# Trunk kernel: Newton steps with one tensor input, and the first weights of a layer subtracted on another engine

## The chip, the cores and the metric

One core of a Trainium2 chip runs the kernel. The engines are TensorE (PE in the profile; its weight loads PEld), VectorE (DVE), ScalarE (ACT), GpSimd (POOL) and SyncE (SP), which issues most of the DMAs. Each works through its own queue in order. The metric is the device time of one execution in microseconds (us); the kernel before has a median of 1444.65 over 3 runs (1443.39 to 1447.72).

## The reference, cut to what matters

Two decoder layers over 512 tokens of width 1024, batch 1, with a layer norm ahead of them:

```python
def layer_norm(x, g, b):
    mu = jnp.mean(xf, axis=-1, keepdims=True)
    xc = xf - mu
    var = jnp.mean(xc * xc, axis=-1, keepdims=True)
    return xc * lax.rsqrt(var + LN_EPS) * g + b

h = layer_norm(x, ln0_g, ln0_b)
for l in range(DEPTH):
    mix = hybrid_mixer(h, w_in[l], ...)
    h = layer_norm(DEEPNORM_ALPHA * h + mix, ln1_g[l], ln1_b[l])
    xa = memory_cross_attention(h, mem, w_xq[l], w_xkv[l], w_xo[l])
    h = layer_norm(DEEPNORM_ALPHA * h + xa, ln2_g[l], ln2_b[l])
    ff = swiglu(h, w_ffn_in[l], w_ffn_out[l])
    h = layer_norm(DEEPNORM_ALPHA * h + ff, ln3_g[l], ln3_b[l])
```

The mixer projects h to a gated causal convolution (31 taps on 512 channels, then a norm) and to a gated linear attention in chunks of 64 tokens (q, k, v, an output gate r and a decay). The cross-attention takes keys and values from 256 memory tokens, which are the same for both layers. All of it is float32.

## The kernel before

**Precision by halves.** A float32 product is made of three matmuls (`mm3`, L136 to L139): each operand is split into a rounded part and what is left of it. `split` (L100) makes the two: ScalarE copies the rounded part (L101), and VectorE or GpSimd subtracts it from the source (L102). Matmuls L137 and L139 need the rounded part of the activations, L138 their remainder.

**Weights.** `wchunk` (L121) loads 512 KB into one of four `raw` buffers by a DMA from SyncE's queue (L125), and splits it into one of four buffers of a ring (`w_...`). ScalarE's copy therefore waits for the DMA and for TensorE to have left the ring's buffer; the next DMA into the same `raw` buffer waits for the subtraction. Which engine subtracts comes from a list that `wlo_engines` sets and `wlo_next` goes through in turn: (POOL, DVE) at first, POOL from the start of a layer's mixer, (POOL, DVE) again from the middle of it, DVE from the cross-attention on.

**Activations.** Four token tiles h_100 to h_103 of 128 tokens. `out_proj` (L254) multiplies into PSUM banks `po`, adds them to h (L273; this frees the bank), takes statistics (L277) and calls `layer_norm` (L175), which takes the mean off (L184), finds the reciprocal root of the variance, scales (L190), and has TensorE transpose the tile (`lt_ln`, L198) into PSUM; `split` then makes hT_ln, which all projections of the next stage read.

**The reciprocal root.** `rstd_of` (L141) starts from an integer trick (L147) and makes five VectorE steps on numbers with n columns: L154, L157, L154, L159, L160. In the layer norms n is 1, one number for each of 128 partitions, and all five are SCALAR_TENSOR_TENSOR with two tensors in SBUF. In the norm of the attention (n = 8) and that of the convolution (n = 2), L151 and L152 stand for L154.

**A layer's mixer** (loop over l, L539 on). `conv_in(0)` projects the first half of the convolution's channels, in layer 1 in two halves of the tokens, so that its first half needs only h_100 and h_101. Its weights are w_c, four chunks (w_c_100, 101, 110, 111 in layer 1), and its first four matmuls go to four banks; two of them were those of the last h. Then come `conv_taps` (L590: 31 taps per channel tile on VectorE, put behind everything else that is ready, so that they fill its gaps), the decays, `conv_in(1)`, q, k and v, the state S, and `gla_pair` for two token tiles at a time: products `pa`, `po`, the norm (y_rms), og on VectorE (L786) and its transposes `ogt` (L790). `conv_norm` transposes the finished taps (acc, cvt) and normalises them. In layer 0 the memory's keys (`mem_K`, w_xk, KT) come ahead of the layer, beside the input norm; in layer 1 between v and the output gate (pair 0) and behind it (pairs 1 to 3). `mem_V` (w_xv) and the output projection (w_mo) follow.

**The input norm** leaves its gain and bias out of h at first: L525 transposes the plain h, and ScalarE applies the gain on the way to hT_ln (xf, L527). `residual0` (L530) later applies them to h itself, on GpSimd, ahead of v in layer 0.

**The order.** It isn't written by hand. Each engine's queue is set when the program is built, by a planner that simulates how long instructions take; `high_priority` moves a stretch forward. An edit in one place can thus reorder others.

Of the kernel before, what the change touches and what calls it, by code (L numbers as in the profile page):

```python
# [12 lines left out]
F32 = mybir.dt.float32  # L13
# [4 lines left out]
ALU = mybir.AluOpType  # L18
AX = mybir.AxisListType

P = 128
# [3 lines left out]
NT = T // P  # L25
# [26 lines left out]
def trunk(ctx: ExitStack, tc, a, out):  # L52
# [53 lines left out]
    def wlo_engines(*engs):  # L106
        wlo[0], wlo[1] = engs, 0
# [33 lines left out]
    def rstd_of(v, n, name):  # L141


        y = small.tile([P, n], F32, tag=f"ny{n}", name=f"y_{name}")
        t = small.tile([P, n], F32, tag=f"nt{n}", name=f"t_{name}")
        s = small.tile([P, n], F32, tag=f"ns{n}", name=f"s_{name}")
        DVE.tensor_scalar(y.bitcast(I32), v.bitcast(I32), -0.5, 1597463007.0 - 2.0 ** 31, ALU.mult, ALU.add)  # L147

        def vyy():
            if n > 1:  # L150
                DVE.tensor_mul(t, y, v)  # L151
                DVE.tensor_mul(t, t, y)  # L152
            else:
                DVE.scalar_tensor_tensor(t, y, v, y, ALU.mult, ALU.mult)  # L154

        vyy()
        DVE.scalar_tensor_tensor(y, t, -3.0, y, ALU.add, ALU.mult)  # L157
        vyy()
        DVE.scalar_tensor_tensor(s, t, -40.0 / 3.0, t, ALU.add, ALU.mult)  # L159
        DVE.scalar_tensor_tensor(y, s, 80.0, y, ALU.add, ALU.mult)  # L160
        return y

    def bcast_row(dst, src_row, n, q):
# [2 lines left out]
    def load_gb(g, b, name, q=nc.sync):  # L166
        gb = block([P, 2, D], F32, f"gb_{name}")
        bcast_row(gb[:, 0, :], g, D, q)
        bcast_row(gb[:, 1, :], b, D, q)
        return gb  # L170
# [301 lines left out]
    def new_K(l):  # L472
        return [block([P, NK, MEM], F32R, f"KT{j}_{l}") for j in range(2)]

    def mem_K(l, mT, KT, pr):
        proj_feat(a["w_xkv"][l], mT,
                  [(pr * 256, 256, lambda m, ps: split(KT[0][:, pr * 2 + m, :], KT[1][:, pr * 2 + m, :], ps))],
                  f"xk{pr}_{l}", n=MEM)
# [10 lines left out]
    def load_x(*tts):  # L489
        for tt in tts:  # L490
            nc.sync.dma_start(h[tt], a["x"][0, tt * P:(tt + 1) * P, :])
# [7 lines left out]
    lncol = const.tile([P, 2 * NK], F32, name="lncol")  # L499
    DVE.tensor_copy(lncol, pl[:, :2 * NK])  # L500
    KT = new_K(0)
    mem_K(0, mT, KT, 0)
    load_x(0, 1)
    mem_K(0, mT, KT, 1)
    load_x(2, 3)
# [21 lines left out]
            ACT.activation(xf, pt, AF.Identity, scale=lncol[:, k:k + 1], bias=lncol[:, NK + k:NK + k + 1])  # L527
            split(hT[0][k // 4][:, k % 4, :], hT[1][k // 4][:, k % 4, :], xf)

    def residual0():  # L530
        gb = load_gb(a["ln0_g"], a["ln0_b"], "ln0")
        for tt in range(NT):
            POOL.tensor_mul(h[tt], h[tt], gb[:, 0, :])
            POOL.tensor_add(h[tt], h[tt], gb[:, 1, :])

# [3 lines left out]
    for l in range(L):  # L539
# [14 lines left out]
        DVE.tensor_scalar(nba, chan[:, 0:2, CW + 3], -1.0, None, ALU.mult)  # L554
        gnorm = chan[:, 0, CW + 4:CW + 5]
        mov = mov_hT(hT)
        wlo_engines(POOL)


        u = block([P, 4, T], F32, n_("u"))  # L560
# [73 lines left out]
            DVE.tensor_copy(dec, qe[:, :, CH - 1::CH])  # L634

        conv_in(0)
        if l > 0:
            mT = mem_T(f"{l}")
            KT = new_K(l)
# [13 lines left out]
        for hp in range(2):  # L653
            pt = bank(n_(f"kdt{hp}"), tag="tr")
            for tt in range(NT):
                PE.transpose(pt[:, tt * P:(tt + 1) * P], kd[:, hp, tt * P:(tt + 1) * P], ident)
            ACT.activation(kdT[:, hp].rearrange("p a b -> p (a b)"), pt, AF.Copy)
        if l == 0:
            residual0()
        v = block([P, NT, 512], F32, n_("v"))  # L660
        run(proj_tok(w_in, mov, 1536, lambda tt, ps: ACT.activation(v[:, tt, :], ps, AF.Copy), n_("v")))

        S = block([P, NCH, 2, P], F32, n_("S"))
        for g in range(2):
            pus = [bank(n_(f"pu{g}{ci}"), tag="tr").rearrange("p (c h e) -> p c h e", c=2, h=2) for ci in range(2)]
# [126 lines left out]

        V = new_V(l)
        if l > 0:
            mem_K(l, mT, KT, 0)
        gla_pair(0)
        run(proj_r)
        wlo_engines(POOL, DVE)  # L800
        for pr in range(1, 4) if l > 0 else ():
            mem_K(l, mT, KT, pr)
        for c in range(2):
# [125 lines left out]
```

## Time and profile before

| | |
|---|---|
| median of 3 runs | 1444.65 us |
| the profiled execution | 1448.14 us |
| its span | 1446.4 us |
| TensorE's mean granted clock | 0.992 |
| TensorE's clock, 720 to 740 us | 0.74 |
| TensorE's clock, 860 to 880 us | 0.91 |
| VectorE busy, 700 to 720 us | 18.50 of 20 us |
| VectorE busy, 820 to 840 us | 20.00 of 20 us |

Layer 0 begins at about 38 us, layer 1 at about 722. A row of a timeline gives start, duration, engine, line, operation, tiles and shapes, how many instructions it groups (x), and in brackets the idle time of the engine before it with what ended it. Numbers in tiles' names are left out in such rows. The granted clock is the share of full speed that TensorE's throttle let through.

### The profile page before, as it was taken

How to read it: one execution, taken by the hardware profiler on the slowest of the kernel's cores; microseconds unless marked ns; L12 is line 12 of the kernel's file. 1: busy time of each engine (PE TensorE's matmuls, PEld its weight loads, DVE VectorE, ACT ScalarE, POOL GpSimd, SP SyncE). 2: the span in 40 equal slices, each digit the busy share in tenths (PEclk: the TensorE clock that was granted, in tenths of full speed). 3: DMA queues.
4: the chain of work that ended last, by engine and by line, in shares of the span. 5: the costliest groups of instructions: out<-in, count | busy, mean ns of one | idle time of the engine just before them, and what ended most of it. 6: DMA issues, size and time to landing. Idle time of an engine off the chain costs nothing.

```text
span 1446.4 us, 22112 instructions
## 1 busy us (share of the span) xinstructions
PE 1405.3 (97%) x8943; PEld 1257.2 (87%) x8943; DVE 1015.9 (70%) x1674; ACT 608.8 (42%) x976; POOL 218.8 (15%) x124
## 2 busy tenths in 40 slices
PE   8999999999999999999979999999999999999997
PEld 7787878988999899899877888889889998998996
DVE  6699977557877367466859997685578664763767
ACT  5553362442555155245225335424424542561550
POOL 3467230000000000000133423300000000000000
PEclk9999999999999999999989999999999999999999
DMA  7423250221365265545242323612214662643641
GB/s 248 131 79 117 88 190 25 95 86 58 97 161 170 76 168 131 147 113 128 84 126 84 93 85 115 217 59 88 76 51 119 164 190 59 161 135 114 146 132 58
DMA packets 108730, 168.62 MB, mean 117 GB/s; under 512 B 7485, under 2 KB 81937, under 8 KB 108629
## 3 DMA queue, kind: packets, MB, share of 16 engines
q1 hardware_dynamic: 102548, 145.98, 32.1%
q0 software_dynamic: 5760, 20.97, 7.8%
q8 instruction: 70, 1.15, 0.3%
q14 instruction: 32, 0.25, 0.1%
q10 hardware_dynamic: 320, 0.27, 0.1%
HBM read 144.13 MB, written 2.10 MB: 101 GB/s over the span
## 4 chain that ended last, share of the span: by engine, by line
PE 76%; DVE 14%; DMA 5%; ACT 3%; issue 2%; POOL 0%; SPq 0%; DVEq 0%; POOLq 0%; ACTq 0%
DVE cv L590 6%; PE po_fo L137 5%; PE po_fo L138 5%; PE po_fo L139 5%; PE fx L402 5%; PE fx L404 5%; PE fx L403 5%; DMA s<-raw_a 3%; PE fw L404 2%; PE fw L403 2%; PE fw L402 2%; PE pp_xq L137 2%; PE pp_xq L138 2%; PE pp_xq L139 2%; PE po_mo L139 2%
## 5 line engine op out<-in xcount | busy, mean ns | idle before, releaser
L284 POOL DMA_DIRECT2D s<-raw_a x40 | 34.9, 885 | 873.4 <-DVE w_s L102 256.1
L590 DVE SCALAR_TENSOR_TENSOR cv<-u,chan,cv 128x511 f32<-128x511 f32 (+28 forms) x240 | 158.6, 728 | 0.3
L138 PE MATMUL po_fo<-w_fo,ph 128*128 128x512 f32 (+1 forms) x358 | 138.1, 386 | 0.0
L139 PE MATMUL po_fo<-w_fo,pl 128*128 128x512 f32 (+1 forms) x358 | 137.0, 386 | 0.0
L137 PE MATMUL po_fo<-w_fo,ph 128*128 128x512 f32 (+1 forms) x358 | 131.7, 386 | 0.0
L101 ACT ACTIVATE w_a<-raw_a 128x1024 fp32r<-128x1024 f32 x60 | 63.2, 1054 | 150.6 <-PE po_fo L139 124.6
L102 DVE TENSOR_TENSOR w_s<-s,w_s 128x1024 fp32r<-128x1024 f32 x80 | 97.3, 1220 | 33.3 <-ACT w_s L101 33.0
L101 ACT ACTIVATE w_s<-s 128x1024 fp32r<-128x1024 f32 x80 | 83.8, 1052 | 48.0 <-DMA s<-raw_a 27.6
L402 PE MATMUL fx<-T_ln,w_s 128*128 128x256 f32 x320 | 91.6, 287 | 3.5 <-ACT u L415 3.3
L403 PE MATMUL fx<-T_ln,w_s 128*128 128x256 f32 x320 | 91.2, 285 | 0.0
L404 PE MATMUL fx<-T_ln,w_s 128*128 128x256 f32 x320 | 90.6, 285 | 0.0
L273 DVE SCALAR_TENSOR_TENSOR h<-h,po_fo 128x512 f32<-128x512 f32 (+1 forms) x49 | 32.3, 671 | 71.2 <-PE po_fo L139 71.1
L102 DVE TENSOR_TENSOR w_a<-raw_a,w_a 128x1024 fp32r<-128x1024 f32 x60 | 73.0, 1220 | 9.1 <-ACT w_a L101 8.1
L139 PEld LDWEIGHTS po_fo<-w_fo,pl 128*128 128x128 f32 x358 | 67.3, 188 | 13.3
L138 PEld LDWEIGHTS po_fo<-w_fo,ph 128*128 128x128 f32 x358 | 67.3, 188 | 13.0
L137 PEld LDWEIGHTS po_fo<-w_fo,ph 128*128 128x128 f32 x358 | 66.9, 188 | 12.9
L402 PEld LDWEIGHTS fx<-T_ln,w_s 128*128 128x128 f32 x320 | 62.2, 194 | 4.2 <-ACT u L415 3.7
L102 DVE TENSOR_TENSOR w_fo<-raw_fo,w_fo 128x1024 fp32r<-128x1024 f32 x44 | 52.8, 1219 | 13.6 <-ACT w_fo L101 13.6
L403 PEld LDWEIGHTS fx<-T_ln,w_s 128*128 128x128 f32 x320 | 62.2, 194 | 0.0
L404 PEld LDWEIGHTS fx<-T_ln,w_s 128*128 128x128 f32 x320 | 61.8, 194 | 0.0
L138 PE MATMUL pp_xq<-hT_ln,w_xq 128*128 128x256 f32 (+1 forms) x192 | 61.3, 322 | 0.0
L139 PE MATMUL pp_xq<-hT_ln,w_xq 128*128 128x256 f32 (+1 forms) x192 | 60.3, 319 | 0.0
(315 smaller groups left out, 4478.3 us busy)
## 6 DMA issues: line engine op xcount, KB each, us to landing
raw_a<-w_ffn_in SPq DMA_DIRECT2D x60, 512.0 KB
raw_fo<-w_ffn_out SPq DMA_DIRECT2D x44, 512.0 KB
s<-raw_a POOLq DMA_DIRECT2D x40, 512.0 KB, 4.9
s<-w_ffn_in SPq DMA_DIRECT2D x20, 512.0 KB
raw_xk<-w_xkv SPq DMA_DIRECT2D x16, 512.0 KB
raw_c<-w_in SPq DMA_DIRECT2D x16, 512.0 KB
raw_xv<-w_xkv SPq DMA_DIRECT2D x16, 512.0 KB
raw_mo<-w_mix_out SPq DMA_DIRECT2D x16, 512.0 KB
```

The lines of the kernel that those rows point to most:

```text
L101: ACT.activation(hi, src, AF.Copy)
L102: eng.tensor_sub(lo, src, f(hi))
L137: PE.matmul(o, lh, rh, start=start, stop=False)
L138: PE.matmul(o, lh, rl, start=False, stop=False)
L139: PE.matmul(o, ll, rh, start=False, stop=stop)
L273: DVE.scalar_tensor_tensor(h[tt][:, c0:c1], h[tt][:, c0:c1], scale, bks[c][:, :c1 - c0], ALU.mult, ALU.add)
L284: POOL.dma_start(dst, src, accum_op=ALU.add)
L402: PE.matmul(o, wh, bh, start=start and k == 0, stop=False, skip_group_check=True)
L403: PE.matmul(o, wh, bl, start=False, stop=False, skip_group_check=True)
L404: PE.matmul(o, wl, bh, start=False, stop=stop and k == 3, skip_group_check=True)
L590: DVE.scalar_tensor_tensor(cv[ct][:, s:], u[:, ct, :T - s], wj, cv[ct][:, s:], ALU.mult, ALU.add)
```

## The change

Line numbers behind L154 grow by 6, behind L502 by 8, and later by up to 17; L157 and L159 are now L160 for n = 1, L190 is L196, L273 is L279, L590 is L602.

1. For n = 1 the five Newton steps become TENSOR_SCALAR: one tensor, and the second as a number per partition.
2. The first chunk of layer 0's first w_xk and the four chunks of `conv_in(0)` of each layer are subtracted on VectorE. `conv_in(1)`, q, k and v stay with GpSimd.
3. In layer 1 VectorE alone subtracts from `mem_K` pair 0 on: w_xk, w_r, w_xv and w_mo. In layer 0 these stay as they were.
4. `residual0` takes tile numbers and is called once ahead of v for tiles 0 and 1 and once behind it for 2 and 3; the block of v is taken ahead of that of the gain.

GpSimd's subtractions and residual steps of 128x1024 go from 128 in all to 102.

```diff
             else:
-                DVE.scalar_tensor_tensor(t, y, v, y, ALU.mult, ALU.mult)
+                DVE.tensor_scalar(t, y, v, y, ALU.mult, ALU.mult)
+
+        def step(o, x, c, z):
+            if n > 1:
+                DVE.scalar_tensor_tensor(o, x, c, z, ALU.add, ALU.mult)
+            else:
+                DVE.tensor_scalar(o, x, c, z, ALU.add, ALU.mult)
 
         vyy()
-        DVE.scalar_tensor_tensor(y, t, -3.0, y, ALU.add, ALU.mult)
+        step(y, t, -3.0, y)
         vyy()
-        DVE.scalar_tensor_tensor(s, t, -40.0 / 3.0, t, ALU.add, ALU.mult)
-        DVE.scalar_tensor_tensor(y, s, 80.0, y, ALU.add, ALU.mult)
+        step(s, t, -40.0 / 3.0, t)
+        step(y, s, 80.0, y)
...
+    wlo_engines(DVE)
     mem_K(0, mT, KT, 0)
+    wlo_engines(POOL, DVE)
...
-    def residual0():
-        gb = load_gb(a["ln0_g"], a["ln0_b"], "ln0")
-        for tt in range(NT):
+    def residual0(*tts):
...
-        wlo_engines(POOL)
+        wlo_engines(DVE)
...
         conv_in(0)
+        wlo_engines(POOL)
...
+        v = block([P, NT, 512], F32, n_("v"))
         if l == 0:
-            residual0()
-        v = block([P, NT, 512], F32, n_("v"))
+            residual0(0, 1)
...
+        if l == 0:
+            residual0(2, 3)
...
         if l > 0:
+            wlo_engines(DVE)
             mem_K(l, mT, KT, 0)
         gla_pair(0)
         run(proj_r)
-        wlo_engines(POOL, DVE)
+        if l == 0:
+            wlo_engines(POOL, DVE)
```

VectorE's queue between the layers, before, from the second subtraction for hT_ln of token tile 0 (lt_ln_00_1) to the first of tile 1 (lt_ln_01_0) and a row on; y_ln_02, t_ln_02 and s_ln_02 are the Newton steps of tile 2:

```order
L102 TENSOR_TENSOR hT_ln_0_6550<-lt_ln_00_1_6648,hT_ln_0_6548 128x4x128
L154 SCALAR_TENSOR_TENSOR t_ln_02_6779<-y_ln_02_6778,v_ln_02_6774 128x1
L277 BN_STATS st_fo_03_6841<-h_103 128x6
L157 SCALAR_TENSOR_TENSOR y_ln_02_6778<-t_ln_02_6779,y_ln_02_6778 128x1
L154 SCALAR_TENSOR_TENSOR t_ln_02_6779<-y_ln_02_6778,v_ln_02_6774 128x1
L159 SCALAR_TENSOR_TENSOR s_ln_02_6780<-t_ln_02_6779 128x1
L273 SCALAR_TENSOR_TENSOR h_103<-h_103,po_fo_0_3_1_6804 128x512
L160 SCALAR_TENSOR_TENSOR y_ln_02_6778<-s_ln_02_6780,y_ln_02_6778 128x1
L277 BN_STATS st_fo_03_6841<-h_103 128x6
L190 SCALAR_TENSOR_TENSOR h_102<-h_102,y_ln_02_6778,gb_ln_0_6544 128x512 x2
L102 TENSOR_TENSOR hT_ln_0_6549<-lt_ln_01_0_6714,hT_ln_0_6547 128x4x128
L178 BN_AGGR mv_ln_03_6846<-st_fo_03_6841 128x2
```

The same stretch in the changed kernel:

```order
L102 TENSOR_TENSOR hT_ln_0_6550<-lt_ln_00_1_6648,hT_ln_0_6548 128x4x128
L102 TENSOR_TENSOR w_c_100_6903<-raw_c_100_6901,w_c_100_6903 128x1024
L102 TENSOR_TENSOR w_c_101_6908<-raw_c_101_6906,w_c_101_6908 128x1024
L154 TENSOR_SCALAR t_ln_02_6779<-y_ln_02_6778,v_ln_02_6774 128x1
L102 TENSOR_TENSOR w_c_110_6915<-raw_c_110_6913,w_c_110_6915 128x1024
L279 SCALAR_TENSOR_TENSOR h_103<-h_103,po_fo_0_3_1_6804 128x512
L102 TENSOR_TENSOR hT_ln_0_6549<-lt_ln_01_0_6714,hT_ln_0_6547 128x4x128
L102 TENSOR_TENSOR hT_ln_0_6550<-lt_ln_01_1_6722,hT_ln_0_6548 128x4x128
L160 TENSOR_SCALAR y_ln_02_6778<-t_ln_02_6779,y_ln_02_6778 128x1
L283 BN_STATS st_fo_03_6841<-h_103 128x6
L102 TENSOR_TENSOR w_c_111_6920<-raw_c_111_6918,w_c_111_6920 128x1024
```

Three of the four Newton steps of tile 2 and its scaling (L190) have moved behind the two subtractions for tile 1, and three weight subtractions stand in their place; the second half of h_103 is behind those. TensorE's queue moves with it: in the kernel before, the transposes of tile 2 (lt_ln_02) stand right behind the first four matmuls of `conv_in(0)`, in the changed kernel 70 matmuls later. The last transposes (lt_ln_03) stand at the end of the first half of the tokens in the changed kernel, and some 30 matmuls ahead of it in the one before.

ScalarE's queue at the start of layer 0, before, from the first w_c copy (w_c_000) to the third (w_c_010); xf_491 and xf_500 are the first two channel tiles of hT_ln:

```order
L101 ACTIVATE w_c_000_586<-raw_c_000_584 128x1024
L101 ACTIVATE KT_0_144<-pp_xk_000_288 128x256
L101 ACTIVATE KT_0_144<-pp_xk_001_289 128x256
L527 ACTIVATE xf_491<-lt_ln_0_486,lncol 128x512
L527 ACTIVATE xf_500<-lt_ln_1_495,lncol 128x512
L101 ACTIVATE w_c_001_591<-raw_c_001_589 128x1024
L101 ACTIVATE hT_ln_406<-xf_491 128x512
L101 ACTIVATE hT_ln_406<-xf_500 128x512
L101 ACTIVATE KT_0_144<-pp_xk_000_352 128x256
L101 ACTIVATE w_c_010_598<-raw_c_010_596 128x1024
```

The same place in the changed kernel, from the copies of KT on:

```order
L101 ACTIVATE KT_0_144<-pp_xk_000_288 128x256
L101 ACTIVATE KT_0_144<-pp_xk_001_289 128x256
L101 ACTIVATE w_c_001_591<-raw_c_001_589 128x1024
L101 ACTIVATE w_c_010_598<-raw_c_010_596 128x1024
L535 ACTIVATE xf_491<-lt_ln_0_486,lncol 128x512
L535 ACTIVATE xf_500<-lt_ln_1_495,lncol 128x512
L101 ACTIVATE KT_0_144<-pp_xk_000_352 128x256
L101 ACTIVATE hT_ln_406<-xf_491 128x512
L101 ACTIVATE KT_0_144<-pp_xk_001_353 128x256
L101 ACTIVATE w_c_011_603<-raw_c_011_601 128x1024
L101 ACTIVATE hT_ln_406<-xf_500 128x512
```

The second and the third copy of w_c have moved ahead of xf. GpSimd's and SyncE's queues keep their order here.

VectorE's queue in layer 1 among the taps of the second half, before (cv_1_7398 and cv_1_7399 are the two channel tiles):

```order
L590 SCALAR_TENSOR_TENSOR cv_1_7398<-u_6893,chan,cv_1_7398 128x505
L590 SCALAR_TENSOR_TENSOR cv_1_7399<-u_6893,chan,cv_1_7399 128x505
L590 SCALAR_TENSOR_TENSOR cv_1_7398<-u_6893,chan,cv_1_7398 128x504
L590 SCALAR_TENSOR_TENSOR cv_1_7399<-u_6893,chan,cv_1_7399 128x504
L590 SCALAR_TENSOR_TENSOR cv_1_7398<-u_6893,chan,cv_1_7398 128x503
L590 SCALAR_TENSOR_TENSOR cv_1_7399<-u_6893,chan,cv_1_7399 128x503
```

At the same tap in the changed kernel:

```order
L602 SCALAR_TENSOR_TENSOR cv_1_7398<-u_6893,chan,cv_1_7398 128x505
L602 SCALAR_TENSOR_TENSOR cv_1_7399<-u_6893,chan,cv_1_7399 128x505
L102 TENSOR_TENSOR w_xk_100_7782<-raw_xk_100_7780,w_xk_100_7782 128x1024
L602 SCALAR_TENSOR_TENSOR cv_1_7398<-u_6893,chan,cv_1_7398 128x504
L602 SCALAR_TENSOR_TENSOR cv_1_7399<-u_6893,chan,cv_1_7399 128x504
L602 SCALAR_TENSOR_TENSOR cv_1_7398<-u_6893,chan,cv_1_7398 128x503
L102 TENSOR_TENSOR w_xk_101_7787<-raw_xk_101_7785,w_xk_101_7787 128x1024
L602 SCALAR_TENSOR_TENSOR cv_1_7399<-u_6893,chan,cv_1_7399 128x503
L602 SCALAR_TENSOR_TENSOR cv_1_7398<-u_6893,chan,cv_1_7398 128x502
```

Up to the last tap eleven such subtractions have come in: the w_xk chunks of all pairs but the very last and the four of w_r. On TensorE the transposes of the taps (cvt) stand behind 85 matmuls of pp_xk instead of ahead of them, and those of og (ogt) behind all of pairs 1 to 3 instead of behind 38 matmuls. SyncE's queue is the same but for the two DMAs of layer 1's gain and bias of the first norm, which come three w_mo loads later.

More of the change, by code (lines that the diff above doesn't have):

```diff
@@ L528, in trunk @@
             split(hT[0][k // 4][:, k % 4, :], hT[1][k // 4][:, k % 4, :], xf)
-    def residual0():
-        gb = load_gb(a["ln0_g"], a["ln0_b"], "ln0")
-        for tt in range(NT):
+    gb0 = []
+    def residual0(*tts):
+        if not gb0:
+            gb0.append(load_gb(a["ln0_g"], a["ln0_b"], "ln0"))
+        gb, = gb0
+        for tt in tts:
             POOL.tensor_mul(h[tt], h[tt], gb[:, 0, :])
```

## The prediction

> **What bounds the kernel now.** I read the page's engine shares first, then what TensorE waited for, then the timelines of the stretches in which those waits lie.
>
> ```profile
> PE 1405.3 (97%) x8943; PEld 1257.2 (87%) x8943; DVE 1015.9 (70%) x1674; ACT 608.8 (42%) x976; POOL 218.8 (15%) x124
> ```
>
> TensorE is busy for 1405.3 of the span's 1446.4 us. The change touches no matmul, so all it can win lies in the 41 us that are left, and it can lose anything by making TensorE wait. What ended TensorE's waits (total, times, longest):
>
> ```profile
> PE lt_ln L198 <- DVE hT_ln L102: 4.0, 1, 4.0
> PE pp_c L137 <- DVE h L273: 3.8, 1, 3.8
> PE ogt L790 <- DVE og L786: 3.3, 1, 3.3
> ...
> PE pp_c L138 <- DVE hT_ln L102: 2.9, 2, 1.7
> ```
>
> These 14.0 us are all VectorE being late. The timeline of VectorE and of GpSimd between the layers shows why; the second column is the duration:
>
> ```profile
> 719.13 0.21 DVE L154 SCALAR_TENSOR_TENSOR t_ln<-y_ln,v_ln 128x1 f32<-128x1 f32 x1
> ...
> 719.86 1.86 DVE L157 SCALAR_TENSOR_TENSOR y_ln<-t_ln,y_ln 128x1 f32<-128x1 f32 x1
> 721.76 2.28 DVE L154 SCALAR_TENSOR_TENSOR t_ln<-y_ln,v_ln 128x1 f32<-128x1 f32 x1
> 724.07 2.27 DVE L159 SCALAR_TENSOR_TENSOR s_ln<-t_ln 128x1 f32<-128x1 f32 x1
> 726.26 0.67 DVE L273 SCALAR_TENSOR_TENSOR h<-h,po_fo 128x512 f32<-128x512 f32 x1
> 726.86 2.15 DVE L160 SCALAR_TENSOR_TENSOR y_ln<-s_ln,y_ln 128x1 f32<-128x1 f32 x1
> ...
> 730.85 0.68 DVE L102 TENSOR_TENSOR hT_ln<-lt_ln,hT_ln 128x512 fp32r<-128x512 f32 x1
> ```
> ```profile
> 719.31 7.01 POOL L102 TENSOR_TENSOR w_c<-raw_c,w_c 128x1024 fp32r<-128x1024 f32 x3 [49.04 <-DVE hT_ln L102]
> 726.65 2.34 POOL L102 TENSOR_TENSOR w_c<-raw_c,w_c 128x1024 fp32r<-128x1024 f32 x1 [0.33 <-ACT w_c L101]
> ```
>
> A Newton step on one number per partition takes 0.21 us alone and 1.86 to 2.28 us while GpSimd subtracts weights: each ends when a GpSimd subtraction ends (726.32 the third, 728.99 the fourth). The two shut each other out. The step at 726.26, which frees a PSUM bank, and the subtraction of hT_ln at 730.85 stand behind them in VectorE's queue, and TensorE stands behind those:
>
> ```profile
> 722.60 0.62 PE L137 MATMUL pp_c<-hT_ln,w_c 128*128 128x256 f32 x3 [0.25 <-ACT hT_ln L101]
> 726.99 0.58 PE L137 MATMUL pp_c<-hT_ln,w_c 128*128 128x256 f32 x1 [3.77 <-DVE h L273]
> 731.58 1.12 PE L198 MATMUL lt_ln<-ident,h 128*128 128x128 f32 x4 [4.01 <-DVE hT_ln L102]
> 732.35 0.56 PE L138 MATMUL pp_c<-hT_ln,w_c 128*128 128x256 f32 x1
> ...
> 735.70 0.41 PE L139 MATMUL pp_c<-hT_ln,w_c 128*128 128x256 f32 x1
> 735.91 0.41 PE L137 MATMUL pp_c<-hT_ln,w_c 128*128 128x256 f32 x1
> ```
>
> After the two waits the matmuls start 0.21 us apart until about 736.5: the wait also cost TensorE its clock.
>
> **The change, part by part.** The sum goes against the profiled execution's 1448.14 us; the median of the three runs, 1444.65, is 3.5 us lower, and I take that off at the end.
>
> *Between the layers.* GpSimd's four subtractions go to VectorE, so nothing shuts the Newton steps out. At 719.13 VectorE had done the first half of h_103 and both subtractions for hT_ln of the first token tile, and by the new order it has done the same by then. Ahead of the second half of h_103 it still has a statistics step (0.60 from start to start), two small ones (0.1) and three of the four weight subtractions. One of these on VectorE, undisturbed, is the 1.23 us of w_xk at 864.95, quoted below; rows overlap by 0.07 to 0.08 (the row at 726.26 ends behind the start of the next), so they come 1.15 apart, 3.45. With 0.3 as an allowance for h_103's first bank, whose wait has moved forward, the second half of h_103 runs at 723.6 to 724.3 instead of 726.26 to 726.93. The two subtractions of 0.6 for the second token tile follow, to 724.9 and 725.5. In the new order TensorE doesn't transpose h_102 here but 70 matmuls later, so it flows from 725.0 instead of 731.58, 6.6 us, and does those transposes later at the full clock, 0.3. Its clock stays up: some 20 matmuls between 732.35 and 736.5 were 0.21 apart instead of the 0.12 of the rows at 871.38 and 871.50 (below), 1.8 more. Against that, h_102 is normalised about 1 us later (to 731.9 instead of 730.85), which is needed only at 733.4, 70 matmuls on. The last transposes (h_103) stand at the very end of the first half, so the second half waits for one copy of hT_ln, 0.6. Sum **-8.1**; from -4 (half of the first wait remains, and the clock falls once) to -10 (nothing waits).
>
> *The start of layer 0.* Here the same four subtractions move, and VectorE's order has them ahead of hT_ln.
>
> ```profile
> 16.03 0.27 DVE L147 TENSOR_SCALAR y_ln<-v_ln 128x1 int32<-128x1 int32 x2
> ...
> 38.16 5.24 DVE L102 TENSOR_TENSOR hT_ln<-xf,hT_ln 128x512 fp32r<-128x512 f32 x2 [4.57 <-ACT hT_ln L101]
> ```
> ```profile
> 14.71 2.39 POOL L102 TENSOR_TENSOR w_xk<-raw_xk,w_xk 128x1024 fp32r<-128x1024 f32 x1 [3.17 <-ACT w_xk L101]
> ...
> 37.68 7.97 POOL L102 TENSOR_TENSOR w_c<-raw_c,w_c 128x1024 fp32r<-128x1024 f32 x3 [2.68 <-PE lt_ln L525]
> ```
> ```profile
> 40.65 0.51 PE L138 MATMUL pp_c<-hT_ln,w_c 128*128 128x512 f32 x1 [1.74 <-DVE hT_ln L102]
> ...
> 43.45 0.50 PE L138 MATMUL pp_c<-hT_ln,w_c 128*128 128x512 f32 x1 [1.14 <-DVE hT_ln L102]
> ```
> ```profile
> 33.87 1.45 ACT L527 ACTIVATE xf<-lt_ln,lncol 128x512 f32<-128x512 f32 x2 [0.80 <-PE lt_ln L525]
> 36.54 1.06 ACT L101 ACTIVATE w_c<-raw_c 128x1024 fp32r<-128x1024 f32 x1 [1.23 <-DMA raw_c<-w_in]
> ```
>
> Two subtractions of hT_ln took 5.24 us instead of 1.36, and TensorE's waits of 1.74 and 1.14 come from it. They would go, 2.9 us. But ScalarE's order has changed too: the copies of the second and third w_c chunk now stand ahead of xf. The second waited for its transfer until 36.54, and nothing brings that transfer forward; so xf comes after 38.6 instead of 33.87, the two copies of hT_ln end at 40.9 and 42.9, the second subtraction at 44.1, and TensorE is where it was at 43.45 some 0.7 us later. Sum **+1**, from -3 (the transfers land earlier) to +4 (they land late, and the clock falls).
>
> A price for the new Newton step is in these rows: TENSOR_SCALAR on 128x1, two in 0.27 us, while GpSimd ran from 14.71 to 17.10. It isn't shut out. But layer 1 has a TENSOR_SCALAR on 128x2 at 871.62 that is:
>
> ```profile
> 861.62 1.34 DVE L590 SCALAR_TENSOR_TENSOR cv<-u,chan,cv 128x482 f32<-128x482 f32 x2
> 864.95 1.23 DVE L102 TENSOR_TENSOR w_xk<-raw_xk,w_xk 128x1024 fp32r<-128x1024 f32 x1 [1.99 <-ACT w_xk L101]
> ...
> 871.62 2.08 DVE L709 TENSOR_SCALAR v<-mv 128x2 f32<-128x2 f32 x1
> 873.61 1.63 DVE L786 SCALAR_TENSOR_TENSOR og<-po,y_rms,gr 128x128 f32<-128x128 f32 x6
> ```
> ```profile
> 871.33 2.34 POOL L102 TENSOR_TENSOR w_xk<-raw_xk,w_xk 128x1024 fp32r<-128x1024 f32 x1 [1.91 <-ACT w_xk L101]
> ```
> ```profile
> 871.38 0.28 PE L137 MATMUL pp_xk<-mT,w_xk 128*128 128x256 f32 x1
> 871.50 0.28 PE L138 MATMUL pp_xk<-mT,w_xk 128*128 128x256 f32 x1
> 875.13 1.06 PE L790 MATMUL ogt<-ident,og 128*128 128x128 f32 x8 [3.35 <-DVE og L786]
> ...
> 877.00 0.41 PE L139 MATMUL pp_xk<-mT,w_xk 128*128 128x256 f32 x1
> 877.22 0.41 PE L137 MATMUL pp_xk<-mT,w_xk 128*128 128x256 f32 x1
> ```
>
> The Trainium skill ("VectorE: DVE Perf Modes", What auto-detection actually checks) says that one source and a destination in SBUF give the two-port mode when their outermost dimensions are both even or equal, and "SBUF — State Buffer" (Who interferes with whom) that this mode takes the port that GpSimd shares. Read so, a 128x1 step would be shut out as well (1 equals 1), the edit would do nothing, and the sum would be 1 us higher, by the steps beside the subtractions that GpSimd keeps at the start. The two rows side by side, 128x2 shut out and 128x1 not, speak for 128x1 staying out of it; I take no loss. Elsewhere the step is worth nothing: in the other norms TensorE is covered, and at the tail five steps of 0.16 to 0.22 may lose 0.1.
>
> *Layer 1, 780 to 945.* The key, value and output weights and the four w_r chunks leave GpSimd. What goes is the stall in the rows above: the 128x2 step was shut out, og finished at 875.2, TensorE stood for 3.35 us, and then ran at 0.21, 1.7 us more if that lasted as long as between the layers: 5.1. What comes is work on VectorE, and it has none to spare here:
>
> ```profile
> 840.00:860.00 20.00, 19.84 (x157) 16.16 (x158) 19.91 (x39) 3.81 (x9) 4.22 (x2) 1.00 0.18 54
> ```
>
> (VectorE's busy time is the third, 19.91 of 20 us.) Eleven more subtractions stand ahead of the last convolution tap, 11 x 1.15 = 12.7 us, and 0.5 of other steps. The last tap ended at 862.96; with all 8.1 us earlier it ends at 868.0. TensorE had done 38 of pp_xk's matmuls at 871.50, so it had begun them at 866.9; 8.1 earlier, and without 0.8 of transposes that now come later, it begins at 858.0. It has 85 of them (10.2 us) ahead of the transposes that need the taps, and reaches these at 868.2; ScalarE's copies of the taps are done about then, or 0.7 later. og, behind two more subtractions and two norm statistics, is done at about 876.5, and TensorE asks for it 59 matmuls and those transposes on, at 876.6 to 877.3. So VectorE is just in time. I take **-4** (1.1 of new waits), from +1 to -5.1. In the output projection GpSimd's four become VectorE's at half the time each; TensorE's order there puts all other work ahead of it, and it didn't wait before: 0.
>
> *Nothing* I give to the residual in halves: GpSimd's rows stand in the same order before and after. If it moved by one GpSimd subtraction (2.40), TensorE's later use of h covers it.
>
> Sum: +1 - 8.1 - 4 + 0 = -11.1, so 1437.0 for an execution like the profiled one, and 1433.5 by the median; I say **1434**.
>
> **The rivals.** *VectorE becomes the bound in layer 1 (slower).* A subtraction waits for ScalarE's copy, and the copy for TensorE to leave a buffer:
>
> ```profile
> 825.71 1.06 ACT L101 ACTIVATE w_xk<-raw_xk 128x1024 fp32r<-128x1024 f32 x1 [1.66 <-PE pt_v L139]
> ```
>
> On GpSimd such a wait held nobody; in VectorE's queue the taps stand behind it. If each of the eleven waits 2 us, the last tap is 22 us later, at 890, and TensorE, at its place at 868.2, loses 21 and 1.7 for the clock: +1 - 8.1 - 5.1 + 22.7 = +10.5, 1455. It is slower than 0.3% from about 1.5 us per subtraction. Against it: those copies run 2 to 3 us ahead of VectorE in my chain. 6%.
>
> *Given back (same).* Four subtractions in front of hT_ln hold VectorE for 4.6 us where GpSimd had taken them. If the start costs 4, the boundary yields only 4, and og comes late by most of its old 3.35, the sum is +4 - 4 - 1.5 = -1.5: 1443. For it: margins of half a microsecond. 14%.
>
> *The steps are shut out all the same*, as the 128x2 step was. GpSimd keeps three subtractions of 2.4 us at the start; steps beside one or two of them hold back the norm by about 1 us, so 1435; elsewhere GpSimd has gone. 10%, inside my case. (This is what the rule of the Trainium skill above would make of it.)
>
> **The numbers.** My forecast has the remaining 80%, the third rival within. About 0.3% (4.3 us) is what a measurement of this kernel can tell from no change: faster below 1440.3. The bounds of the four terms, not all at their ends together, give -16 to -2: 1428.5 to 1443, which leaves out the first rival and the far half of the second.
>
> **What would show it.** Right: Newton steps at 0.15 to 0.2 us between the layers; TensorE's waits on h and hT_ln there under 2.5 us together and no matmuls at 0.21; ogt without its 3.35; the start as long as before. Wrong: a wait of TensorE for acc or og above 3 us near 870, VectorE waiting for w_xk copies between taps, or a start over 4 us longer.

## The result, and the profile after

The changed kernel's median is 1433.07 us, over four executions from 1432.19 to 1433.09; two more, at 1712 and 3552 us, are left out as slow executions, whose cause no run shows. Beside it the kernel before has 1444.76 (six executions, 1443.39 to 1447.96). The ratio is 0.9913, interval 0.9897 to 0.9928. The forecast was 1434. Run again later (c1 below), the changed kernel had 1435.15 beside 1445.46, so the gain is 11.7 us in the first series and 10.3 in the second.

The profiled execution of the changed kernel took 1433.09 us, its span 1431.4, 15.0 less than the one of before. Engine shares, then what ended TensorE's waits (total, times, longest):

```profile
PE 1401.6 (98%) x8943; PEld 1253.1 (88%) x8943; DVE 1024.5 (72%) x1700; ACT 608.2 (42%) x976; POOL 153.5 (11%) x98
```
```profile
PE mt L473 <- DMA mem<-mem: 4.4, 1, 4.4
PE pt_v L137 <- DVE qk L659: 2.0, 1, 2.0
PE lt_ln L533 <- ACT xf L535: 1.8, 1, 1.8
PE pp_c L137 <- DVE h L279: 1.5, 1, 1.5
...
PE pp_c L137 <- ACT hT_ln L101: 0.5, 2, 0.2
...
PE pp_c L138 <- DVE hT_ln L102: 0.2, 1, 0.2
```

Of the four waits on VectorE that the prediction began with (14.0 us), 1.7 are left; ogt is no longer in the list. The first two rows, at the very start and in layer 0, stood in the kernel before too (4.4 and 1.9 us); the third, for xf, is new and lies at the start of layer 0.

Since both kernels issue the same matmuls, the start times of the same matmul in the two traces show where the time went. The stages end at the first `al` of layer 0, the first transpose between the layers, the first `al` of layer 1, its first `pp_qk` with the gate behind it, and its last `po_mo`:

| stage | before, us | after, us | difference | forecast |
|---|---|---|---|---|
| start of layer 0 | 66.04 | 64.33 | -1.7 | +1 |
| layer 0 | 649.85 | 650.70 | +0.8 | 0 |
| between the layers | 43.54 | 36.75 | -6.8 | -8.1 |
| to layer 1's pp_qk | 27.05 | 27.06 | 0 | 0 |
| layer 1's mixer | 179.01 | 173.62 | -5.4 | -4 |
| the rest | 480.9 | 478.9 | -2.0 | -0.1 |

**Between the layers.** VectorE's timeline, then TensorE's (start, duration):

```profile
719.07 2.35 DVE L102 TENSOR_TENSOR w_c<-raw_c,w_c 128x1024 fp32r<-128x1024 f32 x2
721.34 0.27 DVE L154 TENSOR_SCALAR t_ln<-y_ln,v_ln 128x1 f32<-128x1 f32 x1
721.52 1.22 DVE L102 TENSOR_TENSOR w_c<-raw_c,w_c 128x1024 fp32r<-128x1024 f32 x1
722.66 0.68 DVE L279 SCALAR_TENSOR_TENSOR h<-h,po_fo 128x512 f32<-128x512 f32 x1
723.25 1.28 DVE L102 TENSOR_TENSOR hT_ln<-lt_ln,hT_ln 128x512 fp32r<-128x512 f32 x2
```
```profile
723.39 0.39 PE L137 MATMUL pp_c<-hT_ln,w_c 128*128 128x256 f32 x1 [1.47 <-DVE h L279]
723.99 0.39 PE L138 MATMUL pp_c<-hT_ln,w_c 128*128 128x256 f32 x1 [0.21 <-DVE hT_ln L102]
...
725.39 0.42 PE L139 MATMUL pp_c<-hT_ln,w_c 128*128 128x256 f32 x1
725.61 0.41 PE L138 MATMUL pp_c<-hT_ln,w_c 128*128 128x256 f32 x1
```

The steps take 0.2 to 0.3 us and no subtraction stretches them. What still holds TensorE is VectorE's queue: three subtractions of w_c stand ahead of the second half of h_103. And from 725.18 to 728.58 the matmuls are 0.21 apart: the clock still falls once.

**Layer 1.** The same two rows of VectorE as in the prediction, and TensorE's transposes that need og:

```profile
867.77 0.71 DVE L602 SCALAR_TENSOR_TENSOR cv<-u,chan,cv 128x482 f32<-128x482 f32 x1
...
873.56 1.61 DVE L801 SCALAR_TENSOR_TENSOR og<-po,y_rms,gr 128x128 f32<-128x128 f32 x6
875.09 0.16 DVE L724 TENSOR_SCALAR v<-mv 128x2 f32<-128x2 f32 x1
875.15 0.61 DVE L801 SCALAR_TENSOR_TENSOR og<-po,y_rms,gr 128x128 f32<-128x128 f32 x2
```
```profile
877.03 0.40 PE L138 MATMUL pt_xv<-w_xv,mT 128*128 128x512 f32 x1
877.26 1.04 PE L805 MATMUL ogt<-ident,og 128*128 128x128 f32 x8
```

The 128x2 step takes 0.16 us instead of 2.08, the last tap ends at 868.48, og is done at 875.76 and asked for at 877.26: VectorE is in time by 1.5 us.

**The start.** ScalarE's timeline, and below it the same instructions in a second profile of the very same kernel (1429.77 us):

```profile
35.26 1.06 ACT L101 ACTIVATE w_c<-raw_c 128x1024 fp32r<-128x1024 f32 x1 [2.26 <-DMA raw_c<-w_in]
36.77 1.06 ACT L101 ACTIVATE w_c<-raw_c 128x1024 fp32r<-128x1024 f32 x1 [0.46 <-PE pp_xk L139]
37.74 1.43 ACT L535 ACTIVATE xf<-lt_ln,lncol 128x512 f32<-128x512 f32 x2
```
```profile
33.39 1.06 ACT L101 ACTIVATE w_c<-raw_c 128x1024 fp32r<-128x1024 f32 x1 [2.08 <-DMA raw_c<-w_in]
34.92 1.06 ACT L101 ACTIVATE w_c<-raw_c 128x1024 fp32r<-128x1024 f32 x1 [0.47 <-DMA raw_c<-w_in]
35.88 1.43 ACT L535 ACTIVATE xf<-lt_ln,lncol 128x512 f32<-128x512 f32 x2
```

xf stands behind the two copies, as forecast, and TensorE now waits for it (1.8 us). But the transfer landed at 35.26 in one execution and at 33.39 in the other, where the profile before had 36.54.

### The profile page after: what moved, and what is told of

It is laid out like the page before. It is cut to its first block, busy times and chain, and to the rows that moved or that the text cites. A ratio compares the mean times of both kernels' runs of the same rounds, so it can differ in the third digit from the quotient of the medians.

```text
span 1431.4 us, 22112 instructions
## 1 busy us (share of the span) xinstructions
PE 1401.6 (98%) x8943; PEld 1253.1 (88%) x8943; DVE 1024.5 (72%) x1700; ACT 608.2 (42%) x976; POOL 153.5 (11%) x98
## 4 chain that ended last, share of the span: by engine, by line
PE 87%; DVE 5%; DMA 3%; ACT 3%; issue 1%; POOL 0%; SPq 0%; DVEq 0%; POOLq 0%; ACTq 0%
PE po_fo L137 5%; PE po_fo L139 5%; PE po_fo L138 5%; PE fx L408 5%; PE fx L409 5%; PE fx L410 5%; PE fw L410 2%; PE fw L409 2%; PE fw L408 2%; PE pp_xq L137 2%; PE pp_xq L138 2%; PE pp_xq L139 2%; DMA s<-raw_a 2%; PE po_xo L138 2%; PE po_xo L139 2%; PE po_xo L137 2%
## 5 line engine op out<-in xcount | busy, mean ns | idle before, releaser
L602 DVE SCALAR_TENSOR_TENSOR cv<-u,chan,cv 128x511 f32<-128x511 f32 (+28 forms) x240 | 159.7, 730 | 0.3
L279 DVE SCALAR_TENSOR_TENSOR h<-h,po_fo 128x512 f32<-128x512 f32 (+1 forms) x49 | 32.3, 673 | 71.2 <-PE po_fo L139 71.2
L138 PEld LDWEIGHTS po_fo<-w_fo,ph 128*128 128x128 f32 x358 | 67.3, 188 | 13.1
```

Source lines behind the costliest of these rows:

```text
L138: PE.matmul(o, lh, rl, start=False, stop=False)
L279: DVE.scalar_tensor_tensor(h[tt][:, c0:c1], h[tt][:, c0:c1], scale, bks[c][:, :c1 - c0], ALU.mult, ALU.add)
L602: DVE.scalar_tensor_tensor(cv[ct][:, s:], u[:, ct, :T - s], wj, cv[ct][:, s:], ALU.mult, ALU.add)
```

## The experiments

Three theories. T1: what was lost was a mutual lock, between VectorE instructions that read two tensors from SBUF (or the 128x2 step) and GpSimd's subtractions; a 128x1 step with one tensor stays out of it. T2: that step is shut out too, and all the gain comes from the subtractions that left GpSimd. T3: nothing was locked that mattered; weights are ready earlier, because VectorE subtracts in 1.22 us what takes GpSimd 2.4. The kernels were measured in three groups of four, each on a chip of its own and beside the kernel before: e1 to e4 (before: 1444.27 us), e7 to e10 (1444.86), and c1, e6, e10 again and e11 (1445.46). Medians of different groups are best compared by their ratios.

| kernel | median, us | ratio (interval) | start | between | layer 1 |
|---|---|---|---|---|---|
| before (profiled) | | | 66.04 | 43.54 | 179.01 |
| e1, steps alone | 1440.09 | 0.9968 (0.9956 to 0.9979) | 66.75 | 34.61 | 180.09 |
| e2, engines alone | 1435.62 | 0.9940 (0.9929 to 0.9952) | 65.70 | 36.54 | 173.37 |
| e9, steps 128x2 | 1447.99 | 1.0022 (1.0013 to 1.0032) | 66.27 | 42.08 | 179.03 |
| e3, layer 1 as before | 1436.40 | 0.9946 (0.9932 to 0.9959) | 62.54 | 35.26 | 179.15 |
| e8, layer 1 alone | 1440.00 | 0.9966 (0.9954 to 0.9978) | 65.64 | 43.93 | 173.39 |
| e7, all on VectorE | 1481.02 | 1.0253 (1.0235 to 1.0272) | 66.29 | 34.69 | 190.39 |
| e4, w_c on GpSimd | 1434.23 | 0.9923 (0.9909 to 0.9938) | 66.60 | 34.62 | 173.95 |
| c1, changed again | 1435.15 | 0.9924 (0.9906 to 0.9942) | 62.48 | 36.76 | 173.39 |
| e6, layer 0's w_c on GpSimd | 1433.17 | 0.9912 (0.9896 to 0.9928) | 65.39 | 36.75 | 173.82 |
| e10, layer 1's w_c two and two | 1430.85 | 0.9898 (0.9883 to 0.9913) | 66.04 | 34.14 | 173.78 |
| e10 again | 1428.16 | 0.9880 (0.9864 to 0.9896) | 63.35 | 34.14 | 173.63 |
| e11, two and two in both layers | 1431.03 | 0.9901 (0.9885 to 0.9917) | 63.81 | 34.14 | 173.33 |

The last three columns are the stages of the table above, from one profile each. "Between" and "layer 1" hardly depend on anything outside them; "start" differs by 3.6 us among five profiles that run the same instructions there (changed, c1, e3 and the two e10: 62.48 to 66.04).

### Steps or subtractions

**e1** is the kernel before with the first hunk of the diff alone, so that GpSimd keeps every subtraction.

```diff
-                DVE.scalar_tensor_tensor(t, y, v, y, ALU.mult, ALU.mult)
+                DVE.tensor_scalar(t, y, v, y, ALU.mult, ALU.mult)
...
+        step(y, t, -3.0, y)
```

> The kernel before with the first edit alone: the five Newton steps on 128x1 as TENSOR_SCALAR, every subtraction where it was. My theory (GpSimd's subtractions shut out VectorE's steps with two tensors in SBUF, and a 128x1 TENSOR_SCALAR is not one of them): the steps between the layers take 0.15 to 0.25 us beside GpSimd's w_c subtractions, TensorE's two waits of 3.8 and 4.0 there go with the low clock behind them, the wait for og near 870 stays; 6 to 10 us faster, about 1437. Rival (the new step is shut out too, and only the moved subtractions helped): the steps still take about 2 us, 1443 to 1446. A second rival (what helped is that VectorE subtracts in half of GpSimd's time, so that weights are ready earlier) also gives 1443 to 1446, with short steps.

**e2** is the changed kernel with the old steps.

```diff
-                DVE.tensor_scalar(t, y, v, y, ALU.mult, ALU.mult)
...
+                DVE.scalar_tensor_tensor(t, y, v, y, ALU.mult, ALU.mult)
...
-        step(y, t, -3.0, y)
+        DVE.scalar_tensor_tensor(y, t, -3.0, y, ALU.add, ALU.mult)
```

> The changed kernel with the old Newton steps: only the subtractions are moved. My theory: GpSimd is silent between the layers and from the keys of layer 1 on, so the old steps run at 0.15 to 0.25 us too and nearly all of the gain is here, 1432 to 1436. Rival (the cheaper step is what wins): 1440 to 1445.

**e9** is e1 with tiles of two columns, the second a copy of the first; VectorE's queue between the layers is that of e1, row by row.

```diff
-        y = small.tile([P, n], F32, tag=f"ny{n}", name=f"y_{name}")
...
+        m = 2 if n == 1 else n
+        y = small.tile([P, m], F32, tag=f"ny{n}", name=f"y_{name}")
...
-                DVE.tensor_scalar(t, y, v, y, ALU.mult, ALU.mult)
+                DVE.tensor_scalar(t, y, v, y[:, 0:1], ALU.mult, ALU.mult)
```

> The kernel before with the new Newton steps alone, their tiles made two columns wide (the second column a copy of the first), so that VectorE's queue between the layers is that of the steps alone (1440.09 us). If it is the shape that lets a 128x1 step through beside a GpSimd subtraction (the 128x2 row at 871.62 took 2.08 us), the 128x2 steps that start beside the four w_c subtractions between the layers take 1.5 to 2.4 us each, the second half of h_103 comes 4 to 6 us later, and the time is that of the kernel before or more: 1444 to 1449. If it is the one tensor input that lets it through, and the 128x2 row at 871.62 was held by something else, the steps take 0.2 to 0.3 us and the time is 1440.

In e1, VectorE between the layers, and GpSimd's subtractions at the same time:

```profile
722.30 0.27 DVE L154 TENSOR_SCALAR t_ln<-y_ln,v_ln 128x1 f32<-128x1 f32 x1
722.60 0.21 DVE L160 TENSOR_SCALAR y_ln<-t_ln,y_ln 128x1 f32<-128x1 f32 x1
723.43 0.69 DVE L279 SCALAR_TENSOR_TENSOR h<-h,po_fo 128x512 f32<-128x512 f32 x1 [0.61 <-PE po_fo L139]
724.03 0.27 DVE L154 TENSOR_SCALAR t_ln<-y_ln,v_ln 128x1 f32<-128x1 f32 x1
...
726.38 5.30 DVE L190 SCALAR_TENSOR_TENSOR h<-h,mv_ln,gb_ln 128x512 f32<-128x512 f32 x2
```
```profile
721.22 7.09 POOL L102 TENSOR_TENSOR w_c<-raw_c,w_c 128x1024 fp32r<-128x1024 f32 x3 [49.04 <-DVE hT_ln L102]
728.52 2.60 POOL L102 TENSOR_TENSOR w_c<-raw_c,w_c 128x1024 fp32r<-128x1024 f32 x1 [0.21 <-ACT w_c L101]
```

In e9:

```profile
721.69 2.01 DVE L149 TENSOR_SCALAR y_ln<-v_ln 128x2 int32<-128x2 int32 x1
...
724.22 1.80 DVE L156 TENSOR_SCALAR t_ln<-y_ln,v_ln 128x2 f32<-128x2 f32 x1
726.06 2.27 DVE L162 TENSOR_SCALAR y_ln<-t_ln,y_ln 128x2 f32<-128x2 f32 x1
728.24 0.68 DVE L281 SCALAR_TENSOR_TENSOR h<-h,po_fo 128x512 f32<-128x512 f32 x1
```
```profile
721.28 7.03 POOL L102 TENSOR_TENSOR w_c<-raw_c,w_c 128x1024 fp32r<-128x1024 f32 x3 [49.05 <-DVE hT_ln L102]
```

With 128x1 the steps run at 0.2 to 0.3 us beside the subtractions; with 128x2 the same steps in the same queue take 1.8 to 2.3 and end with one of them, the second half of h_103 comes at 728.24 instead of 723.43, and the stretch between the layers takes 42.08 us instead of 34.61. T2 falls, and so does T3: in e1 the weights are hardly earlier than before (GpSimd's fourth is done 12.9 us behind the stretch's first transpose, and 13.1 before), and the gain is there. The 5.30 us of L190, which has two tensors from SBUF, are the rest of the lock; they cost e1 one wait of 1.3 us later.

In e2, where GpSimd is silent between the layers, the old steps with two tensors are short as well (mean ns of one is the figure behind the busy time):

```profile
L154 DVE SCALAR_TENSOR_TENSOR t_ln<-y_ln,v_ln 128x1 f32<-128x1 f32 x8 | 1.6, 207 | 0.1
L157 DVE SCALAR_TENSOR_TENSOR y_ln<-t_ln,y_ln 128x1 f32<-128x1 f32 x4 | 0.6, 156 | 0.0
```

The two edits stand in for each other here: either alone brings the stretch down by 7.0 (e2) or 8.9 us (e1), and both together by 6.8. About 1.5 us of what e1 has ahead is a spell of low clock, which e2 (0.66 from 726 to 730 us) and the changed kernel have here and e1 hasn't. By the medians e1 gains only 4.2 us, where its profile gains 8.9 between the layers and loses 1.1 in layer 1. Of the difference the profiled execution of before, 3.9 us above its median of 1444.27, can hold most. e8 below, which has the instructions of before outside layer 1's mixer, suggests where: in its profile the start, layer 0 and the rest are 2.8 us shorter together, and the stretch between the layers is as long (43.93). That is one profile. e9 is 3.1 us slower than before by the median, though its stretch between the layers is 1.5 shorter; where it loses this isn't located. e2 also ran otherwise in layer 0, with a wait of 2.1 us for og that the changed kernel hasn't; that is the nearest thing in its trace to the 2.5 us that it is slower than the changed kernel.

### Layer 1

**e3** is the changed kernel with layer 1's weights from `mem_K` on as before; **e8** is the kernel before with these alone on VectorE.

```diff
         if l > 0:
-            wlo_engines(DVE)
             mem_K(l, mT, KT, 0)
...
-        if l == 0:
-            wlo_engines(POOL, DVE)
+        wlo_engines(POOL, DVE)
```

> The changed kernel with layer 1's key, value, output-gate and output weights back on GpSimd and VectorE as before; steps and first weights stay changed. My theory: the wait of 3.3 us for og near 870 returns with the low clock behind it, 5 to 6.5 us lost, 1438 to 1440. Rival (VectorE has too much to do among the taps, and the move costs there): 1429 to 1433, faster than the changed kernel.

> The kernel before with edit 3 alone: from layer 1's mem_K on, all subtractions on VectorE, old steps, w_c on GpSimd. My theory: the stall between the layers stays (TensorE waits about 8 us at 723 to 732) and the one near 870 goes (ogt without its 3.35), worth 5 to 6.5: 1438 to 1439.5. The theory that the edits hang together (VectorE must first be ahead by what the boundary gains, or the taps come late): a new wait for acc or og near 865 to 885 above 2 us, and 1442 to 1446.

e3 has the stall of the prediction again, on VectorE and then on TensorE:

```profile
858.51 2.12 DVE L724 TENSOR_SCALAR v<-mv 128x2 f32<-128x2 f32 x1
860.54 1.63 DVE L801 SCALAR_TENSOR_TENSOR og<-po,y_rms,gr 128x128 f32<-128x128 f32 x6
```
```profile
862.06 1.30 PE L805 MATMUL ogt<-ident,og 128*128 128x128 f32 x5 [3.35 <-DVE og L801]
```

Whoever subtracts these weights decides layer 1 by itself: every kernel with GpSimd takes 179.0 to 180.1 us there, every one with VectorE 173.3 to 174.0 (e7 apart, where VectorE has all the others too), whether the boundary was mended (changed, e4) or not (e8). The theory that VectorE must first gain its lead at the boundary falls. By the medians the edit is worth 4.9 us (e8) and, on top of the others, 3.3 (1436.40 against 1433.07); against c1, the changed kernel's second series, it is 1.3, with intervals that overlap. The stage, 5.5 us, is the firmer measure.

**e7** carries the first rival further: no subtraction is left on GpSimd.

```diff
...
-    wlo_engines(POOL, DVE)
+    wlo_engines(DVE)
...
         conv_in(0)
-        wlo_engines(POOL)
+        wlo_engines(DVE)
...
```

> The changed kernel with GpSimd subtracting nothing at all: VectorE also takes the weights that GpSimd has left (w_xk of layer 0, conv_in(1), q, k, v of both layers, w_r and w_mo of layer 0). If VectorE has slack for them (its share of the span is 72%), 1431 to 1434. If a subtraction in VectorE's queue holds the taps and products behind it where VectorE is full already (34.6 of 35 us from 110 to 145 us, and 20 of 20 at 820 to 840), which is the rival of the prediction carried further, TensorE waits there for qk, u and acc: some 30 more subtractions of 1.15 us, a third of them in those stretches, +8 to +15: 1441 to 1448.

It takes 1481.02 us, far more than the 1441 to 1448 expected of the rival. What ended TensorE's waits:

```profile
PE cvb L736 <- ACT acc L730: 9.1, 2, 4.7
PE cvt L720 <- ACT acc L604: 8.5, 2, 8.0
...
PE po L775 <- DVE attT L765: 3.0, 1, 3.0
```

And VectorE in layer 0's mixer (its busy time is the third figure):

```profile
140.00:210.00 70.00, 59.61 (x368) 47.90 (x366) 69.22 (x118) 28.39 (x49) 0.00 (x0) 0.93 0.41 136
```

VectorE is busy for 69.22 of 70 us, the taps come late, and TensorE waits for acc. So VectorE can become the bound, as the first rival has it, but by another way. The rival had the taps held by waits for ScalarE's copies; here VectorE hardly stands idle, and the subtractions themselves fill it. In the changed kernel it doesn't wait for copies either (68.34 us busy in the 68.50 up to layer 1's last tap), and it stays on the near side of the bound by its 1.5 us at og.

### The first weights of a layer

**e4** is the changed kernel with `conv_in(0)` of both layers on GpSimd, **e6** with that of layer 0 alone; **c1** is the changed kernel itself, run beside e6, e10 again and e11.

```diff
         mov = mov_hT(hT)
-        wlo_engines(DVE)
+        wlo_engines(POOL)
```

> The changed kernel with the first w_c chunks of both layers back on GpSimd; steps and layer 1's key weights stay changed. My theory: the new steps are not shut out, so the boundary keeps its gain or wins one or two more since VectorE is spared four subtractions; the start has its two waits on hT_ln again (1.7 and 1.1); 1430 to 1435. Rival (the moved w_c subtractions are what freed the boundary): the waits of 3.8 and 4.0 return, 1440 to 1443.

> The changed kernel with layer 0's four w_c chunks back on GpSimd; the boundary and layer 1 as changed. By the prediction's term for the start (the edit costs 1 us there) it is 1 us faster than the changed kernel: 1432. By the profile after (the start of layer 0 came 1.7 us earlier, and TensorE's two waits on hT_ln there are gone), it is 1.5 to 2 us slower: 1434.5 to 1435. If the landing of the transfers sets the start whichever engine subtracts, the two are within 0.7 us of each other.

> The changed kernel itself once more, as the measure for the three that run beside it: 1433.07 with fast runs from 1432.2 to 1433.1, so 1432 to 1434.5; and its start, which differs by 2 to 4 us between profiles of the same instructions, gives how far that is a matter of the run.

e4 is 34.62 us between the layers, 2.1 less than the changed kernel: with the new steps, giving the four w_c chunks to VectorE costs time there, though 1.5 of the 2.1 us is the spell of low clock, which e4 hasn't (e3, with the chunks on VectorE and no such spell, is 35.26). In layer 0 the subtractions of hT_ln are held again beside GpSimd (e6, the first; then e11 below, where GpSimd is done by then):

```profile
39.91 1.62 DVE L102 TENSOR_TENSOR hT_ln<-xf,hT_ln 128x512 fp32r<-128x512 f32 x1
```
```profile
39.46 0.68 DVE L102 TENSOR_TENSOR hT_ln<-xf,hT_ln 128x512 fp32r<-128x512 f32 x1
```

Its worth stays open: the starts of e4 and e6 (66.60, 65.39) lie at or near the upper end of the five others, but e6's median is below c1's, with intervals that overlap. c1 itself ran from 1429.77 to 1438.67.

**e10** gives layer 1's four chunks to both, **e11** those of both layers.

```diff
-        wlo_engines(DVE)
+        wlo_engines(*((DVE,) if l == 0 else (POOL, POOL, DVE, DVE)))
```

> The changed kernel with layer 1's first w_c chunks split between the engines: the first two on GpSimd, the last two on VectorE. With GpSimd done by about 726, the two steps that take the mean off h_103 (2.49 and 2.88 us where GpSimd had all four) run at 0.74, and h_103's second half isn't behind two subtractions of VectorE, as it is in the changed kernel (wait 1.63). TensorE's waits at 718 to 740 come to 1.0 to 1.6 instead of 3.05: 1430.5 to 1432. If either the mean's steps are shut out all the same or the last two chunks hold the second half of h_103, 1433 or more.

> The changed kernel with layer 1's w_c chunks two and two, once more beside the changed kernel on one chip: 1.5 to 2.5 us faster than it by the median if the 1.63 us wait for h_103 and the low clock behind it are what the split saves; within 0.7 us of it if the first comparison (1430.85 against 1433.07, on different chips) was the chip's.

> The split two and two in both layers. At the start of layer 0 VectorE has two subtractions fewer ahead of hT_ln, but those of xf (two tensors in SBUF) stand beside GpSimd's w_c again, and took 2.6 us each in the kernel before: if they are shut out again, 1 to 2 us slower than with the split in layer 1 alone; if GpSimd's two are done before xf comes, 0 to 1 us faster, 1430 to 1431.

TensorE between the layers in e10's second profile, and GpSimd:

```profile
719.37 0.38 PE L137 MATMUL pp_c<-hT_ln,w_c 128*128 128x256 f32 x1 [0.36 <-DVE h L279]
719.97 0.38 PE L138 MATMUL pp_c<-hT_ln,w_c 128*128 128x256 f32 x1 [0.22 <-DVE hT_ln L102]
720.19 0.28 PE L139 MATMUL pp_c<-hT_ln,w_c 128*128 128x256 f32 x1
```
```profile
715.10 5.72 POOL L102 TENSOR_TENSOR w_c<-raw_c,w_c 128x1024 fp32r<-128x1024 f32 x2 [49.04 <-DVE hT_ln L102]
```

The wait for h_103 falls from 1.47 us (the trace's figure; the expectations say 1.63) to 0.36, the clock stays up, and the stretch takes 34.14 us, 2.6 less than in the changed kernel and 1.1 less than in e3. The first 1430.85 overlaps the changed kernel's 1433.07 by the intervals. On the chip on which the changed kernel had 1435.15, e10 had 1428.16, and there the intervals don't meet. These 7.0 us are more than the 1.5 to 2.5 expected and the 2.6 of the stretch; the rest isn't located. e11 brings nothing beyond e10: the same 34.14, and a median 2.9 us higher than e10's beside it, with intervals that overlap.

## Why the prediction held, point by point

**The number: right, in part by luck.** Against the profiled execution the sum was -11.1, to 1437.0. The profile after took 1433.09, 3.9 us less: the start came 2.7 better than its term, the rest of the span 1.9 and layer 1 1.4, while the stretch between the layers came 1.3 worse and layer 0 0.8. The 1434 fits because the 3.5 us by which the profile before lay above its median were taken off, and the profile after lies at its median. The start, layer 0 and the rest differ by 2 us and more between profiles of the same instructions, so the two terms that the runs bear out are those between the layers and in layer 1.

**The bound and the lock: right.** The four waits that the prediction began with came from VectorE, and VectorE was held by GpSimd. e9 against e1 shows the lock with VectorE's order the same and only the shape changed. One reading was too strict: that all that can be won lies in the 41 us in which TensorE isn't busy. Time at a low clock counts as busy, and the same 8943 matmuls were busy for 1401.6 us instead of 1405.3.

**Between the layers, -8.1: right in kind, 1.3 too much.** The step that failed is "Its clock stays up". The second half of h_103 ran when the sum had it (722.66, in a kernel that is 0.9 us ahead at 715; forecast 723.6), and TensorE went on at 723.39. But it had waited for 1.47 us, and then ran at 0.21 for 3.4 us, 16 matmuls. Here is the stretch in the changed kernel and, with the same instructions and the same wait, in e3; the granted clock is the figure behind GpSimd's:

```profile
725.00:728.60 3.60, 3.60 (x20) 3.60 (x20) 3.27 (x10) 1.11 (x3) 0.00 (x0) 0.53 0.62 170
```
```profile
721.00:724.60 3.60, 3.60 (x33) 3.60 (x32) 3.29 (x10) 1.11 (x3) 0.00 (x0) 1.00 0.61 165
```

In e3 the clock didn't fall, and the stretch was 35.26 us, 8.3 less than before. So the term is -6.8 or -8.3, as the clock goes; three of four profiles (changed, c1 and e6 against e3) have the former. The sum also credited all of it to the subtractions that left GpSimd, and called the new step worth nothing elsewhere; e1 shows that the step alone would have done it, and better.

**The new step isn't shut out: right**, and that one row of 0.27 us carried it. The Trainium skill's rule was read as including 128x1 ("VectorE: DVE Perf Modes", What auto-detection actually checks); no run bears that out. The Trainium skill's words there are "outermost non-unit dims both even or equal"; the prediction left out "non-unit", and a 128x1 step, with one number per partition, has no such dimension beside its partitions. The wording that fits is the Trainium skill's in "Advanced Engine Details and Errata" (Mode Summary): both even, or both odd, above one and equal. By it a 128x1 step stays out and a 128x2 step doesn't, and the rows of e1 (0.27) and e9 (1.80) agree.

**Layer 1, -4: right, 1.4 too little.** The chain held (last tap 868.48 against 868.0, pp_xk from 858.67 against 858.0, og at 875.76 against 876.5); the term of 1.1 us for new waits was not needed. The 5.1 of the old stall and its low clock all came.

**The start, +1: order right, size wrong.** The step that failed is "nothing brings that transfer forward": it landed 1.3 us earlier in one profile of the changed kernel and 3.2 in another. Five profiles of the same instructions there spread over 62.48 to 66.04 us, before and its like (e8) have 66.04 and 65.64: a term between -3.6 and +0.4, and one profile on each side couldn't give it.

**What wasn't forecast**: 0.8 us more in layer 0 and 2.0 less in the rest of the span. No run shows either to be the edits' doing, though the fourth edit had no run of its own. In layer 0 both kernels wait 1.95 us for qk. In the changed kernel's profile the clock fell behind this wait (0.57 over the next 3.4 us) and cost 1.6 us; in the profiles of before, c1, e3 and e10, the last three with the changed kernel's instructions in layer 0, it stayed up. Later in the layer the profile before lost 1.3 of this again, where it stood 1.50 us for an activation of u.

The rest of the span has the same wait. In the kernel before, TensorE stood there for u once more, which was behind a transfer:

```profile
1145.31 0.39 PE L402 MATMUL fx<-T_ln,w_s 128*128 128x256 f32 x1 [1.82 <-ACT u L415]
```

The low clock followed (0.61 over the next 3.4 us). In the other profiles this wait is between 0.18 (changed) and 2.3 us (e4), whatever the edit: it goes by the execution, and may be part of the 3.5 us that were taken off for the median.

## What to carry to other kernels

When two engines lock each other out, changing the form of the short instruction can do what moving the long one does, and it leaves the other engine's queue as it is; try them apart before stacking them, since they may be alternatives. A subtraction moved into a queue stands ahead of what follows in it: give each engine only what it finishes before the consumer of that queue is due, as the split of four chunks two and two did. Read a term that hangs on a transfer's landing from several profiles, not from one.

## What the runs showed of the hardware

- A TENSOR_SCALAR of 128x1 beside a GpSimd subtraction takes 0.20 to 0.27 us (e1), of 128x2 1.80 to 2.27 (e9). The lock works both ways: in e10's second profile a GpSimd subtraction that met one of VectorE took 3.35 us instead of 2.41, and that of VectorE 1.70 instead of 1.23.
- Without GpSimd, the new step is slower than the old: 0.20 to 0.27 us for a 128x1 TENSOR_SCALAR with its factor from SBUF, 0.15 to 0.21 for the SCALAR_TENSOR_TENSOR (e2). So the prediction's 0.15 to 0.2 was a little short.
- After the same wait of 1.5 us TensorE lost its clock for 3.4 us in three profiles and not in a fourth. Behind the wait of 1.9 to 2.0 us for qk in layer 0, ten matmuls started in the next 4 us in four profiles (changed, e1, e9, e11) and 16 or 17 in the nine others that have this wait. The Trainium skill ("TensorE: Matmul & The Clock Gate", What's actually happening) has the clock set by a window of about 3.4 us that runs freely, and the length of the spell agrees. The Trainium skill's table there asks for at least one idle window, though, and here waits of 1.5 to 2.0 us were enough; why they are enough in one execution and not in the next, no run shows.
